# A decode-step layer on one core: gate rows in short pieces, decode states in a part of their own, flags between chains

## The chip, the cores and the metric

The kernel runs on one core of one Trainium2 chip. The metric is device time of that core in microseconds (us), lower is better. The core's engines run side by side, each through its own queue in order: TensorE (PE: matmuls; PEld is its weight load), VectorE (DVE), ScalarE (ACT), GpSimd (POOL) and SyncE (SP, which issues the DMA transfers).

## The reference

One inference step of a hybrid layer: a norm, one input projection, two groups of four heads side by side (mLSTM with gates and a running maximum, HGRN2), an output projection, then a SwiGLU feed-forward. It is computed for a prompt of 1024 positions and for 8 decode sequences of 4 positions, which carry states in and out. The part that the change touches, cut to its core:

```python
def _mlstm_chunk(carry, inp):            # one chunk of one head; carry = state
    C, n, m = carry
    q, k, v, ig, lf = inp
    ...
    F = jnp.cumsum(lf, axis=-1)
    a = F + m[..., None]
    D = jnp.where(mask, F[..., :, None] - F[..., None, :] + ig[..., None, :], -jnp.inf)
    m_t = jnp.maximum(a, jnp.max(D, axis=-1))
    w_inter = jnp.exp(a - m_t)
    W = jnp.exp(D - m_t[..., None])
    s_qk = jnp.einsum('bhtk,bhsk->bhts', q, k) * W
    num = w_inter[..., None] * jnp.einsum('bhtk,bhkv->bhtv', q, C) + jnp.einsum('bhts,bhsv->bhtv', s_qk, v)
    den = w_inter * jnp.einsum('bhtk,bhk->bht', q, n) + jnp.sum(s_qk, axis=-1)
    h = num / jnp.maximum(jnp.abs(den), jnp.exp(-m_t))[..., None]
    ...
    C_new = decay[..., None, None] * C + jnp.einsum('bhs,bhsk,bhsv->bhkv', w_last, k, v)

# around it: q, k = silu(causal conv of width 4 of the projection), lf = log_sigmoid of the f gate,
# out = sigmoid(o) * headnorm(h) * norm_g; for the prompt (state 0) and for decode (given state)
```

All of it is float32.

## The kernel before, in words

The 1056 columns (1024 prompt positions and 32 decode columns) are cut in three blocks: block 0 has 256 prompt columns and the 32 decode ones, blocks 1 and 2 have 384 each. The input projection is a list of *units*: one unit is one 128-row slice of the weights for one block. A float32 product is made of three matmuls on split operands (hi·hi L135, lo·hi L136, hi·lo L137), for 8 slices of the contraction. One such slice, three matmuls, is called a *triple* here, so a unit is 8 triples. For each head of the first group and each block there are units q, k, v, o; for the first head a unit for the gates too (at triples 0, 48 and 88). Then come the units of the second group, the output projection, the feed-forward.

Everything that is not a unit is written as a generator: the norm of the input (its multiplication of X by weight and factor is L228, the split into HI and LO is L229 and L225), the gates, the mixing chain of each head and block (`mix_a`), the decode part (`sample_a`). After every second triple and after each unit `hook()` moves each running generator one step on, where `yield n` says how many hooks to wait. All engines' instructions are written in the order in which these steps come, and each engine keeps that order. So the numbers in the tables (GAW for the gates, MAW for the mixing chains) and the `while ... yield 1` waits on entries of `done` set what stands ahead of what.

Names that the change and the prediction use (lines of before):

- `gates`: L301, L302 read the unit's result out of PSUM on ScalarE; L308 to L310 are the logarithm of the sigmoid (L310 needs another activation table, so a table load goes before it); L312 to L329 on VectorE, with the scans L317 and L319; L331 to L333 three exponentials; L334, L335 store rows to HBM; after more hooks the transposes L343 to L345 on TensorE, copied out by L346 and L347.
- `conv_evac`, q and k: L416, L417 read the unit's result (ScalarE), L435 and L437 or L439 keep the last columns, L445 three taps (VectorE), L449 a sigmoid (ScalarE), L450 the product (VectorE).
- `act_evac`: L469 and L470 for o, L472 for v.
- `mix_a`: L517, L519, L521 weights; L526, L530, L533 the scores and two transposes into three PSUM banks, pS, pK and pV; L540, L541, L544 read them; L549 the update of C, L557 and L559 its sum; L564 stores C; L570, L572 the output; L576 to L583 its norm; L588 a transpose back.
- the decode part: L708, L710 load ngS and wiS from HBM, L714 the scores, L717 to L722 their weights, L608 the load of a state, L612 and L613 transposes, L672 the state's product, L644 and L649 its update, L650 its store, L694 the last transpose.

PSUM gives four rotating banks `mx` to all chains and three banks `mm` to the units; a unit can start when its bank was read out. `finish(key)` runs hooks until a generator has ended, which puts the rest of its steps in one place: `conv_evac` does it for the chain of the block before.

## Time and profile before

| | us |
|---|---|
| median of 3 runs | 1394.06 (1393.78 to 1394.09) |
| the profiled execution | 1394.97 |
| its span, first to last instruction | 1392.9 |
| TensorE busy in it | 1337.1 (96%) |
| VectorE, ScalarE, GpSimd busy | 868.0, 558.6, 593.3 |
| mean granted TensorE clock | 0.982 |

A profile row of instructions reads: start, duration (both us), engine, line, operation, output <- input, shapes, how many. What stands in brackets is the time that the engine stood idle before it, and what ended that. A wait row reads: engine, tile and line that waited <- engine, tile and line it waited for, total us, times, longest. In the profiled execution the units of the first head run from the start to about 110 us, those of the other three heads of the first group to about 300 us; the units of the second group end near 550 us.

### The profile page before, as it was taken

How to read it: one execution, taken by the hardware profiler on the slowest of the kernel's cores; microseconds unless marked ns; L12 is line 12 of the kernel's file. 1: busy time of each engine (PE TensorE's matmuls, PEld its weight loads, DVE VectorE, ACT ScalarE, POOL GpSimd, SP SyncE). 2: the span in 40 equal slices, each digit the busy share in tenths (PEclk: the TensorE clock that was granted, in tenths of full speed). 3: DMA queues.
4: the chain of work that ended last, by engine and by line, in shares of the span. 5: the costliest groups of instructions: out<-in, count | busy, mean ns of one | idle time of the engine just before them, and what ended most of it. 6: DMA issues, size and time to landing. Idle time of an engine off the chain costs nothing.

```text
span 1392.9 us, 29377 instructions
## 1 busy us (share of the span) xinstructions
PE 1337.1 (96%) x11600; PEld 1306.0 (94%) x11600; DVE 868.0 (62%) x2060; ACT 558.6 (40%) x1315; POOL 593.3 (43%) x566
## 2 busy tenths in 40 slices
PE   7888999999999999999998999999999999999996
PEld 7778999899999998999998999999999999999995
DVE  7876667664555456644666667666765346777765
ACT  6554434233344334422435445554544341222232
POOL 5223212231222213222437666666666683444434
PEclk9999999999999999999999999999999999999997
DMA  6012122230101013553464666567654278878743
GB/s 226 23 38 60 66 63 74 87 109 17 49 32 49 32 49 116 149 160 109 163 202 171 211 227 250 204 216 254 218 210 168 78 261 321 300 278 295 278 152 125
DMA packets 108881, 212.11 MB, mean 152 GB/s; under 512 B 10800, under 2 KB 63560, under 8 KB 108232
## 3 DMA queue, kind: packets, MB, share of 16 engines
q1 hardware_dynamic: 108312, 209.98, 43.9%
q8 instruction: 91, 1.49, 0.4%
q14 instruction: 46, 0.38, 0.1%
q10 hardware_dynamic: 432, 0.27, 0.1%
HBM read 143.76 MB, written 66.45 MB: 151 GB/s over the span
## 4 chain that ended last, share of the span: by engine, by line
PE 78%; DVE 10%; ACT 4%; DMA 3%; issue 3%; SPq 1%; POOL 0%; POOLq 0%; DVEq 0%; ACTq 0%
PE mx L1260 16%; PE mm L135 9%; PE mm L1260 9%; PE mm L137 9%; PE mm L136 9%; PE mx L1483 8%; PE mm L1483 5%; PE so L1260 3%; PE mx L644 1%; PE mx L775 1%; PE so L1483 1%; DMA rg<-d_ff 1%; ACT HI L229 1%; DVE X L228 1%; DMA X<-d_x 1%
## 5 line engine op out<-in xcount | busy, mean ns | idle before, releaser
L135 PE MATMUL mm<-HI,whi 128*128 128x384 f32 (+2 forms) x1160 | 379.3, 327 | 6.6 <-ACT gA L302 2.9
L137 PE MATMUL mm<-HI,wlo 128*128 128x384 f32 (+2 forms) x1160 | 363.5, 313 | 1.1 <-POOL wlo L97 1.1
L136 PE MATMUL mm<-LO,whi 128*128 128x384 f32 (+2 forms) x1160 | 363.1, 313 | 0.4 <-POOL LO L225 0.2
L135 PEld LDWEIGHTS mm<-HI,whi 128*128 128x128 f32 x1160 | 221.4, 191 | 11.8 <-ACT gA L302 3.2
L137 PEld LDWEIGHTS mm<-HI,wlo 128*128 128x128 f32 x1160 | 221.3, 191 | 1.6 <-POOL wlo L97 1.6
L136 PEld LDWEIGHTS mm<-LO,whi 128*128 128x128 f32 x1160 | 221.7, 191 | 1.1 <-POOL LO L225 0.5
L97 POOL TENSOR_TENSOR wlo<-raw,whi 128x512 fp32r<-128x512 f32 x90 | 118.6, 1328 | 216.1 <-ACT whi L96 171.1
L1189 POOL TENSOR_TENSOR wlo<-S,whi 128x512 fp32r<-128x512 f32 x78 | 110.3, 1420 | 88.2 <-ACT whi L1188 85.2
L1260 PE MATMUL mx<-T,whi 128*128 128x264 f32 x640 | 118.2, 284 | 0.0
L1260 PEld LDWEIGHTS mx<-T,whi 128*128 128x128 f32 x640 | 99.0, 188 | 0.0
L1313 POOL TENSOR_TENSOR LO<-rg,HI 128x528 fp32r<-128x528 f32 x52 | 70.6, 1369 | 65.1 <-ACT HI L1312 65.1
L1260 PE MATMUL mx<-HI,whi 128*128 128x264 f32 x320 | 91.0, 285 | 0.0
L1260 PE MATMUL mx<-HI,wlo 128*128 128x264 f32 x320 | 90.9, 284 | 0.0
L1260 PE MATMUL mx<-T,wlo 128*128 128x264 f32 x320 | 90.9, 284 | 0.0
L1260 PE MATMUL mx<-LO,whi 128*128 128x264 f32 x320 | 90.7, 283 | 0.0
L1401 DVE TENSOR_TENSOR fh<-fr,fh 128x512 fp32r<-128x512 f32 x80 | 66.2, 828 | 35.0 <-ACT fh L1396 34.7
L1487 DVE TENSOR_TENSOR X<-X,mx 128x264 f32<-128x264 f32 x160 | 65.6, 425 | 26.5 <-PE mx L1483 25.9
L1188 ACT ACTIVATE whi<-S 128x512 fp32r<-128x512 f32 x80 | 50.3, 630 | 71.4 <-DVE S L1177 71.3
L1312 ACT ACTIVATE HI<-rg 128x528 fp32r<-128x528 f32 x52 | 32.3, 641 | 104.5 <-PE mx L1483 28.3
L1260 PE MATMUL mm<-HI,wlo 128*128 128x264 f32 x240 | 68.2, 284 | 0.0
L1260 PE MATMUL mm<-HI,whi 128*128 128x264 f32 x240 | 68.2, 284 | 0.0
L1260 PE MATMUL mm<-LO,whi 128*128 128x264 f32 x240 | 67.9, 283 | 0.0
(545 smaller groups left out, 3424.1 us busy)
## 6 DMA issues: line engine op xcount, KB each, us to landing
d_wf<-fh SPq DMA_DIRECT2D x60, 512.0 KB
rg<-d_ff SPq DMA_DIRECT2D x42, 528.0 KB
raw<-in_wA SPq DMA_DIRECT2D x31, 512.0 KB
whi<-d_wf SPq DMA_DIRECT2D x29, 512.0 KB
wlo<-d_wf SPq DMA_DIRECT2D x28, 512.0 KB
raw<-in_wgu SPq DMA_DIRECT2D x24, 512.0 KB
d_ff<-sg SPq DMA_DIRECT2D x40, 264.0 KB
rg<-in_wgu SPq DMA_DIRECT2D x20, 512.0 KB
```

Of the source, the lines that this page charges most:

```text
L97: (nc.gpsimd if pool else nc.vector).tensor_tensor(lo[:, s], raw[:, s], hi[:, s].bitcast(F32), op=OP.subtract)
L135: nc.tensor.matmul(ps[:, :n], wh, rh[:, k, :], start=(k == 0), stop=False)
L136: nc.tensor.matmul(ps[:, :n], wh, rl[:, k, :], start=False, stop=False)
L137: nc.tensor.matmul(ps[:, :n], wl, rh[:, k, :], start=False, stop=(k == nk - 1))
L1188: nc.scalar.activation(hi[:, s], t, AF.Copy)
L1189: (nc.vector if dve else nc.gpsimd).tensor_tensor(lo[:, s], t, hi[:, s].bitcast(F32), op=OP.subtract)
L1260: nc.tensor.matmul(ps[:, :QN], a[:, w], b_[:, kk, c], start=new and kk == 0 and x == 0, stop=kk == 3 and x == 2, skip_group_check=True)
L1312: nc.scalar.activation(h, src, AF.Copy)
L1313: (nc.vector if dve else nc.gpsimd).tensor_tensor(lw, src, h.bitcast(F32), op=OP.subtract)
L1401: nc.vector.tensor_tensor(lw, src, h.bitcast(F32), op=OP.subtract)
L1483: nc.tensor.matmul(ps[:, :QN], a[:, w], b_[k][:, cs], start=new and k == 0 and x == 0, stop=k == 1 and x == 2, skip_group_check=True)
L1487: nc.vector.tensor_tensor(y, y, ps[:, :QN], op=OP.add)
```

## The change

Four things change:

1. `gates`: more `yield`s cut the row work in short pieces, the table GAW is shortened, and the tiles gA and gB get two buffers. Blocks 1 and 2 no longer wait for the first head's chain of the block before at the start of their row work, only ahead of their stores.
2. `conv_evac` no longer finishes the chain of the block before for q of block 2 of the first head; for later heads it finishes the chain just before. Tiles v and go get a buffer more.
3. Chains of `mix_a` are ordered by `done` entries ("pOa", "pHa") and by `hold`, a flag that keeps others from taking banks between L526 and L544. `mix_b` gets such entries too.
4. `sample_a` leaves its state updates (L644, L649, L650) to `updates()`, which loads the eight states a second time (8 loads more on SyncE, 8 copies more on GpSimd, 8 products more on VectorE). It runs later and is finished ahead of the second decode part.
The matmuls are the same 10,286 in both, and TensorE's order is the same from about triple 526 on.

```diff
-    GAW = ((1, 6, 14), (2, 3, 6), (2, 3, 6))
+    GAW = ((1, 2, 10), (2, 2, 5), (2, 2, 5))
...
-            A, B, Cc = (mp.tile([36, 384], F32, tag=x, name=x) for x in ("gA", "gB", "gC"))
+            A, B, Cc = (mp.tile([36, 384], F32, tag=x, name=x, bufs=nb) for x, nb in (("gA", 2), ("gB", 2), ("gC", 1)))
...
-        while b and ("pS", 0, b - 1) not in done:
-            yield 1
         nc.scalar.activation(a, f, AF.Abs)
         nc.scalar.activation(a, a, AF.Exp, scale=-1.0)
+        yield 1
         nc.scalar.activation(a, a, AF.Ln, bias=1.0)
...
         nc.scalar.activation(wl, wl, AF.Exp)
+        while b and ("pS", 0, b - 1) not in done:
+            yield 1
         nc.sync.dma_start(d_bc[:, 0, o0:o0 + npr], ng)
...
-            if kind == "q" and b and (h or b == 2):
-                finish(("pS", h, b - 1))
+            if kind == "q" and h:
+                finish(("pS", (3 * h + b - 1) // 3, (3 * h + b - 1) % 3))
...
+    hold = [0]
+
     def mix_a(h, b):
...
+        while h + b and ("pOa", 3 * h + b - 1) not in done:
+            yield 1
...
         yield w[0]
+        while hold[0]:
+            yield 1
+        hold[0] = 1
         pS, pK, pV = bank(), bank(), bank()
...
+        while h + b and ("pHa", 3 * h + b - 1) not in done:
+            yield 1
         kt = tl("kt", 384, 1)
...
         nc.vector.scalar_tensor_tensor(W[:, :npr], pS[:, :npr], QS, W[:, :npr], op0=OP.mult, op1=OP.mult)
+        hold[0] = 0
...
                 nc.vector.tensor_scalar_mul(vm[:, 0:w], vt[:, 0:w], seqm[:, s:s + 1])
+                if w == 129:
+                    nc.gpsimd.tensor_copy(sts[s][:, :, 128:129], n_io[0][:, 4 * s:4 * s + 4, None])
                 yield 3
...
-            yield 3 if later is None else 2
+            yield 2
...
-                               o["Cs"], (nT, no), scol[:, 1:2], scol[:, 2:3])
-        nc.sync.dma_start(o["ns"], no)
+                               o["Cs"], (nT, no), scol[:, 1:2], scol[:, 2:3], later=("sua",))
...
         if ui == b0_first + 12 * (H - 1) + 8:
+            finish(("sua",))
             start(sample_b(), ("sb",))
```

How this moves instructions, at three places. Rows of the changed kernel carry its own line numbers: in `gates` L318, L321, L328, L329 are L317, L319, L325, L326 of before, and L332, L333 are L328, L329; in `conv_evac` L441, L443, L451, L456 are L435, L437, L445, L450; L476 is L470; in `mix_a` L556, L559, L573, L575, L580 are L541, L544, L557, L559, L564; L736, L738, L739 are L708, L710, L711.

First place, VectorE at triples 64 to 74: the gates of block 0 (tiles AT and C), the readout of o (go) and of q (st), then the norm of block 1 (L228). Before:

```order
L328 TENSOR_TENSOR AT_121<-C 4x256
L329 TENSOR_TENSOR AT_120<-AT_120,C 4x256
L470 TENSOR_SCALAR go<-go 128x288
L435 COPY raw<-hist 128x3
L437 COPY hist<-raw 128x3
L445 SCALAR_TENSOR_TENSOR st<-raw,vec,st 128x384 x3
L450 SCALAR_TENSOR_TENSOR st<-raw,st 128x384
L228 SCALAR_TENSOR_TENSOR X<-X,vec,mx 128x384 x2
L225 TENSOR_TENSOR LO<-X,HI 128x384
L228 SCALAR_TENSOR_TENSOR X<-X,vec,mx 128x384 x4
L225 TENSOR_TENSOR LO<-X,HI 128x384
```

Now, the row of go and what follows it:

```order
L476 TENSOR_SCALAR go<-go 128x288
L312 SCALAR_TENSOR_TENSOR AT_121<-AT_120,AT_121 4x288
L313 COPY C<-mcar 4x1
L318 SCALAR_TENSOR_TENSOR C<-ones,AT_121 4x128 x2
L321 SCALAR_TENSOR_TENSOR C<-AT_121,mcar,AT_120 4x256
L322 COPY mcar<-C 4x1
L328 TENSOR_TENSOR AT_120<-AT_120,C 4x256
L329 TENSOR_TENSOR C<-C 4x256
L441 COPY raw<-hist 128x3
L443 COPY hist<-raw 128x3
L451 SCALAR_TENSOR_TENSOR st<-raw,vec,st 128x384 x3
L456 SCALAR_TENSOR_TENSOR st<-raw,st 128x384
```

L312 to L326 of before have moved behind the readout of go, and L328 and L329 of before behind the conv's L450. A little further, where the last two of the eight L228 stood right behind the conv of k (ck), the rows now are:

```order
L225 TENSOR_TENSOR LO<-X,HI 128x384
L312 SCALAR_TENSOR_TENSOR gB<-gA,gB 4x384
L313 COPY gm<-mcar 4x1
L441 COPY raw<-hist 128x3
L443 COPY hist<-raw 128x3
L451 SCALAR_TENSOR_TENSOR ck<-raw,vec,ck 128x384 x3
L456 SCALAR_TENSOR_TENSOR ck<-raw,ck 128x384
L228 SCALAR_TENSOR_TENSOR X<-X,vec,mx 128x384
L318 SCALAR_TENSOR_TENSOR gC<-ones,gB 4x128 x3
L228 SCALAR_TENSOR_TENSOR X<-X,vec,mx 128x384
L321 SCALAR_TENSOR_TENSOR gm<-gB,mcar,gA 4x384
```

The gates of block 1 (tiles gA, gB, gC) stand among the norm's steps; in before they came after that block's L544.

Second place, VectorE in the second head, the conv of k and the readout of a chain's banks. Before:

```order
L445 SCALAR_TENSOR_TENSOR ck<-raw,vec,ck 128x384 x3
L450 SCALAR_TENSOR_TENSOR ck<-raw,ck 128x384
L583 TENSOR_SCALAR kt<-mx,sm 128x128 x2
L517 SCALAR_TENSOR_TENSOR W<-ngb,cols,cst 128x128 x3
L521 SCALAR_TENSOR_TENSOR qw<-cq,wib 128x384
L541 TENSOR_TENSOR kt<-mx,cols 128x384
L544 SCALAR_TENSOR_TENSOR W<-mx,W 128x384
```

Now:

```order
L441 COPY raw<-hist 128x3
L443 COPY hist<-raw 128x3
L451 SCALAR_TENSOR_TENSOR ck<-raw,vec,ck 128x384 x3
L456 SCALAR_TENSOR_TENSOR ck<-raw,ck 128x384
L556 TENSOR_TENSOR kt<-mx,cols 128x256
L559 SCALAR_TENSOR_TENSOR W<-mx,W 128x256
L608 SCALAR_TENSOR_TENSOR X<-mx,vec,go 128x384
```

The readout of the banks (L541 of before) now follows right behind the conv of another block's k unit, and TensorE's L549, which needs it, comes 8 triples behind that unit's end, not 20.

Third place, SyncE's queue ahead of the decode part. Before:

```order
L564 DMA out_Cp<-C 128x128
L487 DMA ngb<-d_bc 128x256
L488 DMA wib<-d_bc 128x256
L708 DMA ngS<-d_bc 32x32
L710 DMA wiS<-d_bc 128x32
```

Now:

```order
L493 DMA ngb<-d_bc 128x256
L494 DMA wib<-d_bc 128x256
L580 DMA out_Cp<-C 128x128
L736 DMA ngS<-d_bc 32x32
L738 DMA wiS<-d_bc 128x32
```

The store of C belongs to a chain that is written 20 triples later than before, and the loads of the decode part stand right behind it; on TensorE the decode part's scores (L714) now stand ahead of L526, L530 and L533 of the next chain.

More of the change, by code (lines that the diff above doesn't have):

```diff
@@ L238, in tl @@
     def tl(tag, n=384, bufs=2, dt=F32, p=128):
+        bufs = 3 if tag == "go" else bufs
         return mp.tile([p, n], dt, tag=tag, name=tag, bufs=bufs)
@@ L511, in mix_a @@
         while ("gc", b) not in done or ("cv", "k") not in done:
+            yield 1
+        while h + b and ("pOa", 3 * h + b - 1) not in done:
             yield 1
@@ L522, in mix_a @@
         yield w[0]
+        while hold[0]:
+            yield 1
+        hold[0] = 1
         pS, pK, pV = bank(), bank(), bank()
@@ L536, in mix_a @@
             nc.gpsimd.memset(ktm, 0.0)
+        while h + b and ("pHa", 3 * h + b - 1) not in done:
+            yield 1
         kt = tl("kt", 384, 1)
@@ L572, in mix_a @@
                 nc.tensor.matmul(pO[:, c, 0:129], qw[:, s], cin[c], start=False, stop=True)
+        done.add(("pOa", 3 * h + b))
         yield w[5]
@@ L588, in mix_a @@
             nc.tensor.transpose(pH[:, s], hn[:, s], ident)
+        done.add(("pHa", 3 * h + b))
         yield w[8]
@@ L610, in sample_core @@
         fetch(1)
+        while hold[0]:
+            yield 1
         pK, pV = bank(), bank()
@@ L640, in update @@
             st = sts[s]
+            while hold[0]:
+                yield 1
+            hold[0] = 1
             pUs = [bank(), bank()]
@@ L665, in updates @@
                 yield 3
+            if w == 129:
+                nc.sync.dma_start(o["ns"], n_io[1])
         for s in range(SEQS):
@@ L711, in sample_a @@
         nc.sync.dma_start(nT, i["n0T"])
+        while hold[0]:
+            yield 1
         pS = bank()
@@ L749, in mix_b @@
         q, f, k = S["qb", h, b], S["f", h, b], S["kb", h, b]
+        cid = atn[0]
+        while cid > 1 and ("pO", cid - 2) not in done:
+            yield 1
         AT, AD = ATs[atn[0] % 2], ADs[atn[0] % 2]
@@ L810, in mix_b @@
         yield 1
+        while samp and ("sa",) not in done:
+            yield 1
         nc.vector.copy_predicated(AD[:, :ncb, :], mk[0][:, None].to_broadcast([128, ncb, 32]),
@@ L819, in mix_b @@
         if samp:
-            while ("sa",) not in done:
-                yield 1
             nc.vector.tensor_copy(ss_["sk"][:, h, :], kB[:, 256:288])
@@ L876, in mix_b @@
         yield 1
+        while (("pHb", cid - 1) if cid else ("a", H - 1, 2)) not in done:
+            yield 1
         kt = tl("kt", 384, 1)
@@ L911, in mix_b @@
                 nc.tensor.matmul(pO[:, s], qp[:, s], cin[c], start=False, stop=True)
+        done.add(("pO", cid))
         yield 1
@@ L926, in mix_b @@
             nc.tensor.transpose(pH[:, s], hn[:, s], ident)
+        done.add(("pHb", cid))
         yield 1
```

8 lines of the change are left out of this document (5 added, 3 removed).

## The prediction

> **What bounds the kernel now.** I read three views in order. First the windows by stage: microseconds, busy time of each engine with its instruction count, the clock granted to TensorE, the DMA share and GB/s.
>
> ```profile
> 50.00:70.00 20.00, 14.35 (x76) 13.07 (x75) 16.25 (x36) 12.27 (x23) 4.67 (x6) 0.91 0.06 14
> 70.00:120.00 50.00, 39.40 (x235) 37.86 (x233) 34.80 (x85) 27.19 (x60) 16.04 (x20) 0.86 0.17 49
> 120.00:200.00 80.00, 78.88 (x534) 78.52 (x534) 52.09 (x153) 31.19 (x89) 18.62 (x29) 1.00 0.20 63
> 200.00:300.00 100.00, 98.34 (x706) 94.35 (x706) 68.53 (x198) 35.91 (x91) 28.88 (x58) 1.00 0.30 93
> ```
>
> TensorE (first column) sets the time everywhere. From 120 us on it is 98% busy at full clock, so nothing can be won there, but something can be lost. Only 50 to 120 us has slack: 16.3 us of idle, and a lowered clock. Second, the waits from 40 to 125 us: total, times, longest.
>
> ```profile
> PE mx L344 <- ACT gB L332: 4.1, 1, 4.1
> PE mx L572 <- DVE C L557: 3.7, 1, 3.7
> PE mm L135 <- ACT gA L302: 2.9, 1, 2.9
> PE mx L549 <- issue: 1.8, 1, 1.8
> PE mm L135 <- ACT st L417: 1.7, 1, 1.7
> PE mx L530 <- DVE X L228: 1.0, 1, 1.0
> ```
>
> Third, TensorE alone in windows of 2 us, where the second last figures but two give the clock:
>
> ```profile
> 52.00:54.00 2.00, 0.67 (x4) 1.00 0.00 0
> 60.00:62.00 2.00, 0.27 (x1) 1.00 0.44 110
> 64.00:66.00 2.00, 2.00 (x8) 0.50 0.00 0
> 82.00:84.00 2.00, 2.00 (x16) 0.50 0.74 145
> 110.00:112.00 2.00, 1.99 (x11) 0.50 0.66 151
> ```
>
> The 1.7 us wait near 52 us left the clock at 1.00; the idle of 2.9 us and more before 62, 82 and 110 us was each followed by windows at 0.50. A window at 0.50 loses 1 us, and each such spell spans two to three windows: I price it at 2 us.
>
> **The front, triples 72 to 128.** (A triple is L135, L136, L137 for one slice of the contraction; the k-th is counted from the start of the main loop.) The flags and pieces only change the order in which instructions are written, and each engine keeps that order. Here they put the steps of gates on VectorE and ScalarE ahead of work that TensorE waits for, and all later matmuls queue behind a waiting one. Rows of before:
>
> ```profile
> 51.54 0.45 DVE L312 SCALAR_TENSOR_TENSOR AT<-AT,AT 4x288 f32<-4x288 f32 x1 [2.24 <-ACT AT L310]
> 52.83 0.50 ACT L469 ACTIVATE go<-mx,hbo 128x288 f32<-128x288 f32 x1
> 53.99 0.41 DVE L326 TENSOR_TENSOR C<-C 4x256 f32<-4x256 f32 x1
> 55.33 0.31 DVE L470 TENSOR_SCALAR go<-go 128x288 f32<-128x288 f32 x1
> 55.89 1.92 DVE L445 SCALAR_TENSOR_TENSOR st<-raw,vec,st 128x384 f32<-128x384 f32 x3
> 58.47 0.56 DVE L450 SCALAR_TENSOR_TENSOR st<-raw,st 128x384 f32<-128x384 f32 x1 [0.65 <-ACT raw L449]
> 58.94 1.13 DVE L228 SCALAR_TENSOR_TENSOR X<-X,vec,mx 128x384 f32<-128x384 f32 x2
> 59.63 1.00 ACT L229 ACTIVATE HI<-X 128x384 fp32r<-128x384 f32 x2
> 61.11 0.57 ACT L302 ACTIVATE gA<-mm,vec 4x384 f32<-4x384 f32 x1
> ```
>
> Triple 72: L470 now stands ahead of L312 and cannot start before L469 ends at 53.33. So L312 starts at 53.66, L326 ends 2.86 later at 56.5, L445 runs 56.9 to 58.8, L450 ends at 60.0. Then come L328 and L329 (0.85 in before) and the two L228: 60.9 to 62.0. On ScalarE the three exponentials L331 to L333 (some 0.4 each) now stand between the two L229, so L302 ends near 64.9, not 61.7. TensorE, which ran dry at 58.8, idles 6.1 us in place of 2.9: +3.2.
>
> Triple 74: L530 needs the last of the eight L228 (its bank held their factor), and L533 needs L346. In before these wait 1.0 us in all, because the gates of the second block start only later:
>
> ```profile
> 74.02 1.28 ACT L310 ACT_TABLE_LOAD   x1
> 76.52 1.03 DVE L317 TENSOR_TENSOR_SCAN gC<-ones,gB 4x128 f32<-4x128 f32 x3
> 77.48 0.98 DVE L319 TENSOR_TENSOR_SCAN gm<-gB,mcar,gA 4x384 f32<-4x384 f32 x1
> 78.57 0.53 DVE L325 TENSOR_TENSOR gA<-gA,gC 4x384 f32<-4x384 f32 x1
> 80.29 0.55 DVE L329 TENSOR_TENSOR gA<-gA,gC 4x384 f32<-4x384 f32 x1
> ```
>
> Now they come first. ScalarE from 64.9: L229 0.5, L308, L309 0.5 each, L229 0.5, the load 1.3, L310 0.5, L229 0.5: 69.2. VectorE's L225 waits for that; ScalarE goes on with L229, L416, L417 to 70.9, which L445 waits for: to 72.9. A second table load ahead of L449 (1.28), L449 0.53, L450 0.56: 75.2. L228, three L317, L228: 77.4, and L530 goes. L319 to L329 take 78.4 to 80.8 and L346 releases L533 near 81. TensorE reached triple 74 at about 67 (two triples at half clock after 64.9) and stands some 13 us. It leaves triple 74 near 81 against 63 in before, of which 2 us are this chain's own transposes, which before makes later: +16.
>
> From there the change gives back. Before loses after triple 74 the waits for L530, L549 and L572 (6.5 us in the list above) and two spells of half clock: 10.5 us. The new order has its own half clock (2 to 3) and L572 still waits 2 us for L557, now behind L445 and L450. Shift at triple 118: 16 - 10.5 + 5 = +10; added up by absolute times (before passes it at 105.2, after 81 + 44 triples of 0.5 + some 8 of other matmuls and losses) it is +6. I take +7.
>
> Triple 118: L549 waits for L541, which stands behind the gates of the third block, whose L449 has a table load. Rows of that place in before, where a POOL subtraction (L97) runs beside the three scans, which take 3.13 us there and 1.03 above:
>
> ```profile
> 95.40 2.19 ACT L96 ACTIVATE whi<-raw 128x512 fp32r<-128x512 f32 x4
> 96.06 3.13 DVE L317 TENSOR_TENSOR_SCAN gC<-ones,gB 4x128 f32<-4x128 f32 x3
> ```
>
> After the k unit's end the chain L417, L445, load, L449, L450, L317 to L329, L541 is 10.5 us, TensorE has 7.6 us of work, and the four L96 ahead of L416 add up to 3: a stall of 3 to 10, I take 6.5. In its place goes the L344 wait of 4.1. Net +2. **Front: +9**, bounds +4 to +15.
>
> By the Trainium skill ("TensorE: Matmul & The Clock Gate", Part 1: The HAM clock gate) the clock falls only after an idle window of about 3.4 us; here 2.9 us was enough. By the page two stalls near 3 us that I charge with a half clock below would be free, which takes an estimated 4 us off the sum. The same notes ("ScalarE: Activation LUTs", What ACT_TABLE_LOAD costs) add about 1.38 us of drain to every load. The trace shows the next activation right behind the 1.28 us, and the row decides; by the page the two loads ahead of L530 would make it nearly 3 us worse, as an estimate.
>
> **The later chains, triples 150 to 440.** The order flags move each L549 from 20 triples behind its k unit to 8. It waits for L541, behind L445, L449 and L450 of that k unit:
>
> ```profile
> 91.85 0.56 DVE L541 TENSOR_TENSOR kt<-mx,cols 128x384 f32<-128x384 f32 x1 [0.25 <-PE mx L588]
> 219.57 3.03 DVE L445 SCALAR_TENSOR_TENSOR ck<-raw,vec,ck 128x384 f32<-128x384 f32 x3
> ```
>
> L416 to L541 is 1.1 + 1.9 + 0.6 + 0.6 + 0.6 with its gaps, 4.9 us; TensorE has 8 triples and L588, 4.75 us. So 0.15 us each at eight places without POOL, 1.4 us where L97 doubles a step (L445 3.03 in place of 1.92). POOL is busy about a quarter of this stretch: **+4.5**, bounds +1 to +11. Taken out are waits of before: 0.7 and 0.4 at L549 and L572 near 121 us, 0.6 at L694 near 300 us, and
>
> ```profile
> PE mx L572 <- DVE C L557: 1.6, 1, 1.6
> ```
>
> **-3.3.**
>
> **The decode part.** Its loads stand on SyncE's queue behind out_Cp of the third head's last chain, which now comes with the L549 at triple 336, not 316; and L533, now behind the decode part's products at triple 346, waits for the last L721:
>
> ```profile
> 229.78 0.83 PE L549 MATMUL mx<-vt,kt 128*128 128x129 f32 x6
> 232.33 0.34 SPq L564 DMA_DIRECT2D out_Cp<-C  x1
> 236.97 0.42 SPq L710 DMA_DIRECT2D wiS<-d_bc  x1
> 245.66 0.24 DVE L717 SCALAR_TENSOR_TENSOR sW<-ngS,scol,cst 128x32 f32<-128x32 f32 x1
> 247.52 0.19 DVE L722 SCALAR_TENSOR_TENSOR sq<-sq,wiS 128x32 f32<-128x32 f32 x1
> 81.21 0.34 SPq L487 DMA_DIRECT2D ngb<-d_bc  x1
> ```
>
> L549 to out_Cp 2.55, eight issues at 0.465, L717 to the last L721 1.85, and a landing that no row shows: at most the 4.8 us from L487 at 81.21 to the L517 that waited for it, at least nothing; I take 2.5. That is 10.6 us, and TensorE has 7 to 7.5: a stall of 3.2 and 2 of half clock, **+5**, bounds 0 to +9. At triple 362 L613 waits for L541 behind the conv of a k unit that ended two triples earlier: 4.9 - 1.5, some 3.3, and 2 of clock: **+5**, bounds +2 to +7. The L672 with two buffers of st, refilled 8 triples ahead (4 us), **+1.5**, bounds 0 to 6. The moved updates bring 8 loads of 256 KB, 8 copies on POOL and 8 products on VectorE into a stretch where DMA is a third busy and VectorE two thirds: **+1**, bounds -1 to +4. They lie beside TensorE's own work; without that cover the 8 products and 8 copies would cost 4 us. Behind them, from triple 526 on, the order is as before.
>
> **The sum**: 9 - 3.3 + 4.5 + 5 + 5 + 1.5 + 1 = +22.7 on the profiled execution's 1394.97, so 1417.7. The median of the runs is 0.9 lower than that execution: **1417 us**.
>
> **The rivals.** (1) The front alone: the short stalls from triple 150 on are taken up because VectorE and ScalarE run less behind than I chain them. Front +9, removed waits -3.3, and at most 4 of the rest, on 1394: 1400 to 1404, about 1402. For it speaks that the windows from 120 us show VectorE at 65 to 69%; against it that a queue in order passes on every delay. Chance 0.20. (2) The decode part decides: the loads of the state and of wiS queue up, so the landing takes its upper bound (+2.3), st its 6 us (+4.5) and the updates their 4 (+3), 10 more than my sum: 1427 and, with the upper bound of the chains, to 1440. For it speaks that two buffers leave 4 us for a load whose landing no row bounds below 4.8; against it that DMA is a third busy there. Chance for above 1432: 0.10. (3) The other side, faster: the pile-up at triple 88 to 96 was the dear place, and its price is L549 1.8, L572 3.7, L344 4.1 and two half-clock spells of 2, with 1.6 and 0.6 later: 18 us, 1376. It decides if the last L228 is done by 67 us, when TensorE reaches triple 74, that is if the gates of the second block do not get ahead of it on ScalarE and VectorE. The order speaks against it: L310's load and L445 both precede it. If only part of it comes, 1376 to 1391. Chance 0.10. (4) The stalls only move, sum within 2.8 us. Chance 0.05. My forecast, 1408 to 1432 around 1417, has 0.55.
>
> So slower by over 0.2% (2.8 us, about what these runs can tell from no change) has 0.20 + 0.10 + 0.55 = 0.85, within 0.05, faster 0.10. The range 1396 to 1436 leaves out (3), half of (2) and most of (4): 0.10 + 0.05 + 0.04, under 2 in 10.
>
> **What would show it.** Right: a wait of about 10 us for L228 near 67 us with L346 behind it, no wait at L344 near 106 us, a wait for L541 at triple 118, TensorE 7 to 11 us behind at triple 128, then waits for L541 of 0.2 to 1.4 us every 16 us, and one for L721 near 250 us. Wrong: TensorE busy from 67 to 77 us (then rival 3), the windows from 130 to 230 us at 99% (then rival 1), or a gain or loss behind 320 us, where the order is the same.

## The result, and the profile after

The changed kernel takes 1434.4 us (median of 4 runs, 1428.9 to 1435.6) against 1393.9 us: a ratio of 1.028, 95% interval 1.026 to 1.030. It is slower by 40 us. The forecast was 1417 us and slower. The measured time lies outside the forecast's own 1408 to 1432 us and 1.6 us inside the upper end of the stated range of 1396 to 1436. So the sign and most of the places were right, and the size was too small by 17 us. The profiled execution took 1433.76 us, its span is 1431.7.

The same stages in the profile of the changed kernel (us; busy time of PE, PEld, DVE, ACT, POOL with instruction counts; granted clock of TensorE; DMA):

```profile
50.00:70.00 20.00, 12.13 (x63) 11.01 (x61) 10.98 (x26) 13.16 (x23) 3.85 (x5) 0.84 0.07 14
70.00:120.00 50.00, 30.09 (x169) 28.88 (x169) 28.09 (x61) 20.80 (x40) 12.36 (x13) 0.81 0.12 35
120.00:200.00 80.00, 73.53 (x487) 72.36 (x488) 45.85 (x148) 29.20 (x83) 17.94 (x26) 0.95 0.19 60
200.00:300.00 100.00, 88.15 (x566) 85.47 (x565) 53.05 (x162) 30.39 (x85) 19.39 (x36) 0.95 0.17 52
300.00:400.00 100.00, 95.89 (x1041) 89.20 (x1041) 57.62 (x199) 35.23 (x107) 30.27 (x55) 1.00 0.31 93
```

TensorE now idles 20 us between 70 and 120 us, and it is no longer saturated behind 120 us either: 6.5, 11.9 and 4.1 us of idle in the next three windows, and a mean clock of 0.95 in two of them. VectorE is less busy than before in each of the first four windows, ScalarE in three of them. They have not become the bound; their work stands in the wrong order.

TensorE's waits from 40 to 150 us and, behind the dots, from 150 to 620 us (total, times, longest; lines are those of the changed kernel: L543 and L546 are L530 and L533 of before, L556 is L541, L565 is L549, L751 is L721, L632 is L612; L890, a product of the second group, is L858):

```profile
PE mx L543 <- DVE X L228: 10.1, 1, 10.1
PE mx L565 <- DVE kt L556: 9.4, 2, 8.6
PE mx L350 <- ACT AT L336: 3.7, 1, 3.7
PE mx L546 <- DVE cols L352: 3.6, 1, 3.6
PE mx L588 <- DVE C L573: 2.1, 1, 2.1
...
PE mx L890 <- DVE wib L834: 5.8, 6, 2.0
PE mx L565 <- DVE kt L556: 4.9, 5, 1.9
PE mx L546 <- DVE PB L751: 3.6, 1, 3.6
PE mx L565 <- POOL sv L482: 2.9, 2, 1.4
PE mx L632 <- ACT vt L555: 2.7, 1, 2.7
```

Each of the waits that the prediction walked through is there. The first row behind the dots is no new wait: the kernel before waits 4.0 us at the same line. To see what each costs in the end I compare positions and not only waits. TensorE's order of unit matmuls is the same in all kernels here, so the start of the first matmul (L135) of triple k can be compared between two traces, counted from each trace's first instruction. The difference to the kernel before is called the *lag*. It is set to 0 at triple 64, where the change begins to act, because executions differ by up to 2 us ahead of that. (Each of the two traces has 11,600 TensorE instructions, where the text on the change says 10,286 matmuls.) The table is worked out in this way from the traces of the runs (us):

| lag at triple | 72 | 80 | 96 | 112 | 128 | 208 | 336 | 368 | 448 | 524 |
|---|---|---|---|---|---|---|---|---|---|---|
| changed kernel | 3.0 | 18.0 | 11.4 | 8.4 | 15.2 | 17.6 | 25.2 | 31.3 | 30.7 | 38.9 |
| E1 gates back | 0.0 | 0.0 | -9.4 | -2.0 | 4.4 | 5.7 | 11.7 | 17.7 | 17.1 | 25.3 |
| E2 decode back | 3.0 | 17.0 | 10.5 | 7.4 | 13.7 | 16.2 | 23.7 | 31.4 | 43.5 | 44.8 |
| E3 flags alone | 0.0 | 0.0 | -9.4 | -1.3 | 4.4 | 5.7 | 13.2 | 18.9 | 32.1 | 33.4 |
| E4 norm first | 3.0 | 8.6 | 4.0 | 4.2 | 9.5 | 11.9 | 19.5 | 25.1 | 24.6 | 32.8 |
| E5 short tail | 3.0 | 17.9 | 11.4 | 8.4 | 15.1 | 17.5 | 25.2 | 24.1 | 25.9 | 30.7 |
| E6 decode alone | 0.0 | 0.0 | 0.0 | 0.0 | 0.0 | -0.1 | -0.1 | -0.5 | 1.6 | 6.4 |
| E7 repaired | 0.0 | 0.0 | -9.3 | -1.3 | 5.3 | 6.6 | 13.3 | 12.2 | 13.8 | 18.7 |
| E8 wait half filled | 3.0 | 18.2 | 13.2 | 10.1 | 16.3 | 18.8 | 26.3 | 31.7 | 31.2 | 39.4 |
| E9 later transpose | 0.0 | 0.0 | 0.6 | 0.6 | 0.5 | -0.1 | -0.1 | -0.6 | 0.7 | 5.5 |
| E10 tail of 4 | 0.0 | 0.0 | -9.4 | -2.8 | 2.9 | 2.2 | 6.0 | 6.0 | 6.4 | 11.2 |
| E11 both waits filled | 3.0 | 15.6 | 9.0 | 6.0 | 12.4 | 14.8 | 22.4 | 27.9 | 27.3 | 35.4 |

From triple 524 to the end the changed kernel's lag changes by less than 1 us: all of it is made between 55 and 411 us of its trace.

Two cautions go with the table. Each row is one execution: E8, which changes little, differs from the changed kernel by up to 1.8 us in it. And the lag also counts work that has only changed places. Over the whole stretch from triple 64 to 524 the changed kernel and the kernel before do the same matmuls, but at 112, for instance, 18 matmuls of a chain that the kernel before has done are still to come in the changed kernel.

The dearest place, triple 74, in the timeline of the changed kernel (start, duration, engine, line):

```profile
66.78 1.28 ACT L310 ACT_TABLE_LOAD   x1
68.07 0.52 ACT L310 ACTIVATE gB<-gB 4x384 f32<-4x384 f32 x1
...
69.17 0.56 DVE L225 TENSOR_TENSOR LO<-X,HI 128x384 fp32r<-128x384 f32 x1 [4.71 <-ACT HI L229]
71.45 1.92 DVE L451 SCALAR_TENSOR_TENSOR ck<-raw,vec,ck 128x384 f32<-128x384 f32 x3
73.44 1.28 ACT L455 ACT_TABLE_LOAD   x1 [2.72 <-DVE ck L451]
77.26 0.58 DVE L228 SCALAR_TENSOR_TENSOR X<-X,vec,mx 128x384 f32<-128x384 f32 x1
77.89 0.69 PE L543 MATMUL mx<-ident,ck 128*128 128x128 f32 x2 [10.13 <-DVE X L228]
81.33 0.55 DVE L333 TENSOR_TENSOR gA<-gA,gC 4x384 f32<-4x384 f32 x1
82.13 0.69 PE L546 MATMUL mx<-ident,ktm 128*128 128x128 f32 x2 [3.55 <-DVE cols L352]
```

The reader sees the chain of the prediction in order: the gates' logarithm with its table load, the norm's L225 that waited 4.7 us for ScalarE, the conv of k, a second table load for L455 (called a sigmoid above; the kernel writes it with a tanh), the last L228, and TensorE's L543 behind it; then the gates' last VectorE step and L546.

### The profile page after: what moved, and what is told of

The parts are those of the page before. It is cut to its first block, busy times and chain, and to the rows that moved or that the text cites. A ratio compares the mean times of both kernels' runs of the same rounds, so it can differ in the third digit from the quotient of the medians.

```text
span 1431.7 us, 29409 instructions
## 1 busy us (share of the span) xinstructions
PE 1344.0 (94%) x11600; PEld 1310.6 (92%) x11600; DVE 862.0 (60%) x2068; ACT 557.3 (39%) x1315; POOL 594.3 (42%) x574
## 3 DMA queue, kind: packets, MB, share of 16 engines
q8 instruction: 91, 1.49, 0.4%
## 4 chain that ended last, share of the span: by engine, by line
PE 75%; DVE 12%; ACT 6%; issue 3%; DMA 2%; POOL 0%; SPq 0%; POOLq 0%; DVEq 0%; ACTq 0%
PE mx L1296 16%; PE mm L1296 9%; PE mm L135 9%; PE mm L137 8%; PE mx L1519 8%; PE mm L136 8%; PE mm L1519 5%; PE so L1296 3%; DVE ck L451 2%; PE mx L807 1%; PE so L1519 1%; PE mx L667 1%; DMA rg<-d_ff 1%; ACT HI L229 1%; PE mx L565 1%
## 5 line engine op out<-in xcount | busy, mean ns | idle before, releaser
L135 PE MATMUL mm<-HI,whi 128*128 128x384 f32 (+2 forms) x1160 | 382.6, 330 | 3.2 <-ACT gA L303 1.3
L135 PEld LDWEIGHTS mm<-HI,whi 128*128 128x128 f32 x1160 | 223.8, 193 | 9.5 <-issue 3.2
L97 POOL TENSOR_TENSOR wlo<-raw,whi 128x512 fp32r<-128x512 f32 x90 | 117.1, 1314 | 178.1 <-ACT whi L96 175.4
L1523 DVE TENSOR_TENSOR X<-X,mx 128x264 f32<-128x264 f32 x160 | 65.5, 425 | 27.8 <-PE mx L1519 27.3
L504 POOL TENSOR_TENSOR sm<-sm,mhalf 128x3 f32<-128x3 f32 (+2 forms) x26 | 21.3, 818 | 144.1 <-DVE sm L499 50.4
```

The source lines that it names most:

```text
L97: (nc.gpsimd if pool else nc.vector).tensor_tensor(lo[:, s], raw[:, s], hi[:, s].bitcast(F32), op=OP.subtract)
L135: nc.tensor.matmul(ps[:, :n], wh, rh[:, k, :], start=(k == 0), stop=False)
L1523: nc.vector.tensor_tensor(y, y, ps[:, :QN], op=OP.add)
```

## The experiments

E1 to E3 take the change apart. **E1**, the gates as before:

```diff
-    GAW = ((1, 2, 10), (2, 2, 5), (2, 2, 5))
+    GAW = ((1, 6, 14), (2, 3, 6), (2, 3, 6))
...
+        while b and ("pS", 0, b - 1) not in done:
+            yield 1
         nc.scalar.activation(a, f, AF.Abs)
...
-        while b and ("pS", 0, b - 1) not in done:
-            yield 1
         nc.sync.dma_start(d_bc[:, 0, o0:o0 + npr], ng)
```

(and the pieces' `yield`s and the second buffers taken out).

> The changed kernel with the gates written as before (GAW, the pieces, the early wait for pS, one buffer of gA and gB); flags, decode part and conv rule stay changed. In the changed kernel TensorE is 15.0 us behind the kernel before at triple 128, 25.0 at triple 336, 38.8 at triple 524. Theory (the gates' steps stand ahead of the norm's L228 and of L541 on VectorE and ScalarE): the lag at triple 128 falls to 0 to 4 us, the later 24 us stay: 1416 to 1424 us. Rival (the front loss comes from the order flags and from the chain of block 0 no longer being finished early, not from the gates): the lag at triple 128 stays 12 to 15 us, 1430 us or more.

Measured: 1421.8 us, ratio 1.020 (1.017 to 1.022). The wait for L228 is gone and the lag at triple 128 is 4.4 in place of 15.2; the later 21 us stay. That is the theory, 0.4 us beyond its upper number. But the row holds a surprise: at triple 96 this kernel is 9.4 us *ahead* of the one before. Of that, 3.7 us are idle time and 3.0 us half clock that are gone between triples 80 and 96; the rest is 27 matmuls that come only behind triple 96. The likely cause is that the early `finish` ahead of block 2's q is left out (it runs hooks until the scores L526 of the chain before are written, not to the end of that chain); no run takes it out alone. TensorE then loses all of it again. Its waits, and ScalarE's queue at that place (lines of E1: L332 is L331 of before, L550 is L540, L560 is L549):

```profile
PE mx L560 <- ACT vt L550: 8.3, 1, 8.3
PE mx L583 <- DVE C L568: 3.1, 1, 3.1
...
107.56 1.28 ACT L332 ACT_TABLE_LOAD   x1
112.85 0.52 ACT L332 ACTIVATE gB<-gB 4x384 f32<-4x384 f32 x1 [4.01 <-DVE gB L329]
114.49 0.49 ACT L550 ACTIVATE vt<-mx 128x384 f32<-128x384 f32 x1
```

ScalarE stands 4 us at an exponential of the gates of block 2, which waits for VectorE's steps behind the scans, and the readout of vt that TensorE needs stands behind it.

**E2**, the decode part as before:

```diff
-                               o["Cs"], (nT, no), scol[:, 1:2], scol[:, 2:3], later=("sua",))
+                               o["Cs"], (nT, no), scol[:, 1:2], scol[:, 2:3])
+        nc.sync.dma_start(o["ns"], no)
...
-            yield 2
+            yield 3 if later is None else 2
...
-            finish(("sua",))
             start(sample_b(), ("sb",))
```

> The changed kernel with the decode part as before (state updates inside the loop, no second load of the states). Theory (the decode part is a loss of its own, 14 us from triple 336 to 524: the wait of pV for the decode weights, the waits at triple 362, the updates' work in the second group): lag at triple 336 unchanged at 25 us, lag at triple 524 at most 30 us: 1420 to 1426 us. Rival (the chains' new order makes that loss, whoever does the updates): lag at triple 524 stays above 35 us, 1431 us or more.

Measured: 1437.3 us, ratio 1.030 (1.027 to 1.033), not faster. The theory falls. The lag at triple 336 is the same as in the changed kernel within 1.5 us, at 524 it is 6 us more. The loss from 336 to 368 is there with the old decode part too (7.7), so it belongs to something else. Behind 448 the lag now grows by 1.3 in place of 8.2, but it grows by 10 between 416 and 448. The place is triple 440, where `finish(("sa",))` writes what is left of the decode part in one piece: between triples 432 and 448 TensorE does 24 state products (L672) and 24 update products (L644) more than in the kernel before, and stands still for 5.1 us:

```profile
PE so L700 <- POOL st L656: 2.9, 1, 2.9
PE mx L722 <- DVE sjunk L719: 2.2, 1, 2.2
```

(rows of E2 for 328 to 367 us: L700 is L672 of before, L722 is L694.) The late chains make the old decode part late, and what is late is done without cover. So with these chains the new decode part is a small gain by the traces; the intervals of the two ratios overlap.

**E3**, gates and decode part both as before (the edits of E1 and E2 together). What is left of the change are the flags, `hold`, the conv rule and the buffers of v and go.

> The changed kernel with gates and decode part both as before: the flags, the hold, the conv rule and the buffers of v and go are what is left of the change. Theory (three separate losses that add up): only the waits for L541 in the chains are left, 10 us, and 0 to 4 at the front: 1402 to 1409 us. Rival (the losses feed each other, each late queue making the next one late): below 1399 us. Other rival (the flags are the main loss): above 1415 us.

Measured: 1426.1 us, ratio 1.022 (1.020 to 1.025): the rival "the flags are the main loss". Flags, rule and buffers alone cost 32 us of the 40. The gates add 13 (E1 to the changed kernel) or 11 (E3 to E2), and the decode part takes 3 or 4 off (E2 to the changed kernel, E3 to E1; the intervals of both pairs overlap, the lag at 524 is lower by 6 and 8). These four were not run one by one; E5 shows a part of what the order flags do.

**E4**, only the place of the gates of block 1:

```diff
         while b == 0 and ("cv", "k") not in done:
             yield 1
+        while b == 1 and ("n1", 2) not in done:
+            yield 1
         nc.scalar.activation(a, f, AF.Abs)
```

> The changed kernel in which the gates of block 1 start their row work only when the norm of block 2 has written all its steps, so the eight L228 stand ahead of it; nothing else changes. Theory (place in the queue): the 10.1 us wait of TensorE for L228 falls to 3 us or less, the lag at triple 128 from 15 to 3 to 9 us: 1422 to 1428 us. Rival (the same VectorE and ScalarE work must be done before triple 118 anyway, so the stall only moves there): the lag at triple 128 stays 13 us or more, 1432 us or more.

Measured: 1428.0 us, ratio 1.024 (1.022 to 1.026). TensorE's waits:

```profile
PE mx L567 <- DVE kt L558: 13.3, 7, 7.6
...
PE mx L545 <- DVE X L228: 4.9, 1, 4.9
...
PE mx L352 <- ACT AT L338: 3.7, 1, 3.7
```

The wait for L228 falls from 10.1 to 4.9, not to 3 or less, and the wait for L346 (3.6) is gone; the lag at triple 128 falls by 5.7 us and is 9.5, half a us outside the expected 3 to 9. Place in the queue makes half of this wait and all of that for L346; the lag of 3.0 at triple 72, from block 0's gates behind the readout of go, is untouched by this edit. The stall at triple 118 stays (7.6 in place of 8.6), so the work has not simply moved there.

**E5**, one number of the chains' table:

```diff
-        (2, 1, 3, 1, 2, 2, 2, 6, 1))
+        (2, 1, 3, 1, 2, 2, 2, 3, 1))
```

> The changed kernel with one number of MAW changed: in the row for heads 2 to 4 the hooks between the norm of a chain (L583) and its transposes back (L588) are 3, not 6. The transposes set the flag pHa on which the next chain's readout (L541) waits, so L541 is written ahead of the next k conv and L549 goes back to its places in the kernel before from triple 284 on. Theory (the flag puts L541 behind the conv, and so delays every chain by 12 to 20 triples, which also brings the decode weights in front of pV): lag at triple 128 unchanged at 15 us, the waits for L541 between 200 and 336 gone, the wait for L721 at triple 346 gone, lag at triple 368 at 15 to 19 us instead of 31, the updates' part (448 to 524) still +6 to +8: 1415 to 1422 us. Rival (it is the decode part and its loads that make the losses from 336 on, wherever the chains stand): lag grows by 5 us or more between 336 and 368 as before, 1426 us or more.

Measured: 1424.1 us, ratio 1.022 (1.020 to 1.024). Both named waits are gone, that for L721 at triple 346 and that at 362: between triples 336 and 368 the lag now *falls* by 1.1 us, where it grew by 6.1. That part of the theory holds, and it takes the loss there from the decode part and gives it to the late chains. Between 208 and 336 nothing is won (7.7 and 7.6 us), since other waits stand in the place of those for L541:

```profile
PE mx L605 <- DVE kt L600: 3.5, 3, 1.4
PE mx L588 <- DVE C L573: 2.1, 1, 2.1
```

(rows of E5 for 200 to 265 us: L605 is the transpose L588 of before, L600 its norm L583; L588 and L573 are L572 and L557). Three hooks are too few for the norm through VectorE, ScalarE and GpSimd. And a wait of 4.6 us for L691 (sjunk) appears at the decode part's last transpose; it may be why the time is 2 us above the expectation.

**E6**, the decode part's change alone on the kernel before.

```diff
-                               o["Cs"], (nT, no), scol[:, 1:2], scol[:, 2:3])
-        nc.sync.dma_start(o["ns"], no)
+                               o["Cs"], (nT, no), scol[:, 1:2], scol[:, 2:3], later=("sua",))
```

(with the copy of the n column, the store of ns behind the updates and `finish(("sua",))`, as in the change).

> The kernel before with the decode part's change alone: the state updates in a part of their own with 8 more loads of the states; gates, chains and conv rule as before. Theory (the decode part by itself is no loss; its waits come from chains that are late): within 4 us of before, 1391 to 1398 us. Rival (second loads, copies and updates in the second group cost what the prediction's terms for triples 346 to 524 say): 1400 us or more.

Measured: 1401.1 us, ratio 1.0055 (1.0033 to 1.0076): the rival, by a little. The same edit that takes 3 us off among late chains costs 7 among punctual ones. More than half of that, by size, is one wait:

```profile
PE mx L698 <- DVE sjunk L695: 4.6, 1, 4.6
```

**E7**, a try at a repair: E1, the tail of 3, and the gates of block 2 behind the readout of block 1's chain.

```diff
-        while b and ("pS", 0, b - 1) not in done:
+        while b and (("pS", 0, 0) if b == 1 else ("kt", 0, 1)) not in done:
             yield 1
         nc.scalar.activation(a, f, AF.Abs)
...
         hold[0] = 0
+        done.add(("kt", h, b))
         yield w[2]
```

> The changed kernel with gates as in the run with the gates written as before, the short tail of 3 hooks, and one more wait: the gates of block 2 start their row work only when the chain of block 1 has written its readout (L540, L541, L544), so that readout no longer stands behind L331 to L333. Flags, hold and decode part stay changed. Theory: the wait of 8.3 us for vt at triple 124 goes, lag at triple 128 from +4 to -6 to 0 us, the waits for L541 go, what is left is the updates' part: 1392 to 1402 us. Rival (gates of block 2 come too late for their own chain, and the wait moves to L344 or L549 of the next chain): lag at triple 152 at +3 us or more, 1404 us or more.

Measured: 1413.9 us, ratio 1.013 (1.010 to 1.016): the rival. The wait of 8.3 us for vt is gone, and in its place TensorE's L572 (L584 here) waits nearly as long for the next step of the same chain, L559 (L571 here):

```profile
PE mx L584 <- DVE C L571: 7.4, 1, 7.4
```

The gates of block 2 hold VectorE for 8 us in one piece (105.4 to 113.4 us in E1). At both places where they were put between triples 96 and 128, the chain's next step waits for them; the lag at triple 128 is 5.3 with this repair and 4.4 without.

**E8** fills part of TensorE's stand at triple 74 with transposes that nobody reads.

```diff
         done.add(("pS", h, b))
+        if (h, b) == (0, 0):
+            dm = bank("so")
+            for _ in range(30):
+                nc.tensor.transpose(dm[:, 0:128], ident, ident)
```

> The changed kernel with 30 more transposes on TensorE (identity by identity into the unused bank so, read by nobody) between L526 and L530 of the first chain, where TensorE otherwise stands idle for 10 us waiting for L228. Nothing that anyone waits for moves. Theory (an idle stretch halves the clock that is granted after it, and that costs time of its own): the granted clock is at 1.00 again by 78 us, triples 74 to 80 lose 0 to 1 us to the clock in place of 2.5, the lag at triple 80 falls from 17.8 to 14 to 16 us: 1430 to 1433 us. Rival (the clock of this stretch follows something else than TensorE's own idling): the clock stays at 0.50 until about 87 us and the time at 1434 us or more.

Measured: 1432.1 us, ratio 1.028 (1.026 to 1.030). Inconclusive: the 30 transposes ended 4 us before the wait did; the clock rose to 1.00 at 72 us and fell again at 79. It did show what one costs (14 in 1.49 us at full clock), from which the next run is sized.

**E11** fills both waits: 68 of them ahead of L530 and 26 between L530 and L533.

> As the run with 30 more transposes, but with 68 of them between L526 and L530 and 26 between L530 and L533 of the first chain (0.106 us each at full clock, by that run), so that TensorE is busy through nearly all of the two waits for L228 and L346. Theory (the granted clock follows TensorE's own idling, in stretches of 3.4 us): full clock from about 72 us on, no half clock between 75 and 90 us, triples 74 to 80 some 2.5 us shorter, the lag at triple 80 at 14 to 16.5 us in place of 17.8, the later lag lower by as much. Rival: the clock stays low until about 87 us and the lag at triple 80 at 17 us or more.

Measured: 1430.1 us, ratio 1.025 (1.022 to 1.027). TensorE alone in windows of 2 us (busy time, instructions, granted clock), first the changed kernel, then E11:

```profile
74.00:76.00 2.00, 0.00 (x0) 0.50 0.00 0
84.00:86.00 2.00, 2.00 (x8) 0.50 0.27 70
86.00:88.00 2.00, 2.00 (x10) 0.64 0.56 130
```

```profile
74.00:76.00 2.00, 2.00 (x21) 1.00 0.00 0
84.00:86.00 2.00, 2.00 (x13) 1.00 0.22 63
86.00:88.00 2.00, 2.00 (x15) 1.00 0.42 137
```

In the same 2 us TensorE does 13 and 15 matmuls in place of 8 and 10. The lag at triple 80 falls by 2.4 us and stays lower by 2.3 to 3.5 us from there on. The half clock behind a stall is a cost of its own, about what the prediction put on it (2 us a spell). The intervals of the two ratios overlap, so for the whole kernel this difference rests on the traces.

**E9**, E6 with the decode part's last transpose later:

```diff
         nc.vector.tensor_scalar_mul(hn, pO[:, 0:128], sm[:, 2, 0:1])
-        yield 1
+        yield 4
         pH = bank()
```

> The kernel before with the decode part's change alone, and the last transpose of a decode part (L694) three hooks later behind the VectorE step that it needs (L691). Theory (of the 7 us that the decode part alone costs, 4.6 us of wait at this one place and a half-clock spell of 2.5 us are the whole): 1391.5 to 1396 us, no wait at L694 above 0.5 us. Rival (the moved updates and second loads are a cost of their own): 1397.5 us or more.

Measured: 1401.8 us, ratio 1.0053 (1.0033 to 1.0073): the rival. The wait for L691 is gone; the updates' first product (L644) now waits in its place:

```profile
PE mx L644 <- DVE svm L660: 3.6, 1, 3.6
```

The lag grows by 2.6 us between triples 336 and 400 and by 4.8 between 448 and 524, where the moved products now stand. From triple 336 to 524 the matmuls are the same as in the kernel before, so what moved cancels, and what is left is idle time (+3.3 us) and half clock (+2.6). So the decode part's change has a price of its own in the kernel before, 5.5 us by the lag and 7.7 by the medians, and it is not this one wait.

**E10** joins what helped: E1, a tail of 4 hooks (long enough for the norm, short enough that L541 is written ahead of the next k conv in most chains), and E9's later transpose.

> The changed kernel with the gates written as before, 4 hooks in place of 6 ahead of L588 in heads 2 to 4, and L694 three hooks later; flags, hold and decode part stay changed. Theory (parts add: front +4 as with the gates written as before, chains +2 to +4, triples 336 to 368 -1, no wait at L694, updates +5): lag at triple 524 +6 to +11 us: 1400 to 1405 us. Rival (each change of place only hands the wait to the next step, as in the repaired kernel's front): 1411 us or more.

Measured: 1407.5 us, ratio 1.011 (1.009 to 1.013); its profiled execution's lag at triple 524 is 11.2, 0.2 us above the expected span of values. It lies between theory and rival. The chains from triple 128 to 336 cost 3.1 us in place of 10.0, and between 336 and 368 nothing. It is the fastest kernel here with flags, but no version beat the kernel before.

## Why the prediction was right, and where it was short

**The sum.** The prediction had +9 for the front, +3.4 for the chains and +10.3 for triples 336 to 524; measured are 15.2, 10.0 and 13.7. All three parts were too small, and none made up for another. Over the whole stretch, in which the matmuls are the same, TensorE idles 31.8 us more than in the kernel before and loses 5.4 us more to half clock. That the time still lies in the range is in part luck: the prediction gave the band above 1432 us to rival (2) with a chance of 0.10, and what that rival needs did not happen (below).

**The front: place right, size +9 predicted, +15.2 measured.** Triple 72: +3.2 predicted, +3.0; what ends the wait is L302 of before, as predicted (it ends at 64.6, 64.9 predicted), with a wait for an exponential (3.7 us, L350 above) ahead of it that the prediction did not have. Triple 74: waits of 10.4 and 2.6 ("some 13 us") predicted, 10.1 and 3.6 measured. All stalls that the prediction put between triples 64 and 128 add up to 27.6 us (6.1, 13, 2 and 6.5); the trace has 29.6. So the stalls were nearly right, and what was mis-sized is the way from them to the sum. From triple 74 to 118 the prediction counted the shift in two ways, +10 and +6, and took +7. Measured is +8.4 at triple 112 with 18 matmuls still to come, about 2.5 us by an estimate from L565 above (six in 0.9 us), so +10 was the better of the two. At triple 118 a stall of 6.5 was predicted and 8.6 measured; with these 18 matmuls and 0.7 us more of half clock +2 became +6.8 (15.2 - 8.4). L318, the scans, stood under POOL's L97 again (from 115.22 for 2.71 us) and took 2.99 us:

```profile
115.21 2.99 DVE gC L318 x3
118.21 0.92 DVE gm L321
121.53 0.57 DVE kt L556
```

(rows of the critical chain: start, length, what.) E1 and E4 show that the order of the gates makes this part. What the prediction did not see is E1's other half: with the gates as before, the rest of the change is 9.4 us ahead at triple 96, at the place that rival (3) described, and each place of block 2's gates that was tried gives it back by triple 128.

**The chains: +4.5 less 1.1 predicted (the waits of before near 121 us), +10.0 measured** (triples 128 to 336). The mechanism was right, L549 behind the conv of a k unit; the term was mis-sized. TensorE's idle at the seven places between triples 144 and 336 is 0.8, 0.3, 1.9, 1.4, 0.3, 1.9, 1.4: I had said 0.2 to 1.4 each. The two of 1.9 are the k units of block 2, where L445 runs beside POOL's L97 and takes 2.76 us in place of 1.93; the prediction had such places, at 1.4. The two of 0.3 are the k units of block 1, without L97. The other three I had priced like blocks of 384 columns, with 4.75 us of cover. For chains whose k unit is a block 0 unit the cover is eight triples of 288 columns, and behind L423 stand L427, three more taps (L454) and GpSimd copies. One such place in the changed kernel:

```profile
198.24 0.58 ACT L423 ACTIVATE ck<-mm,b,vec 128x288 f32<-128x288 f32 x1
201.46 0.46 DVE L456 SCALAR_TENSOR_TENSOR ck<-raw,ck 128x288 f32<-128x288 f32 x1 [0.57 <-ACT raw L455]
201.83 0.55 DVE L556 TENSOR_TENSOR kt<-mx,cols 128x384 f32<-128x384 f32 x1
202.26 0.21 POOL L482 COPY sv<-v 128x32 f32<-128x32 f32 x1
202.53 0.91 PE L565 MATMUL mx<-vt,kt 128*128 128x129 f32 x6 [1.44 <-POOL sv L482]
```

A spell of half clock near 245 us (1.7) makes up the rest.

**The decode part: places and path right, put down to the wrong edit.** The wait of L533 for L721 was predicted at 3.2 and is 3.6; that at triple 362 was predicted at 3.3 and is 2.7, each followed by a half clock. The path to L721 is the predicted one: the critical chain runs from out_Cp (266.23) over the loads on SyncE's queue to the landing of the last ngS,

```profile
270.38 2.82 DMA ngS<-d_bc
```

2.8 us where I took 2.5. The prediction charged both waits to the decode part. E5 removes both with one number of the chains' table, E2 leaves them in place with the old decode part (its lag from 336 to 368 is 7.7). They belong to the flags, which write L549 of most chains 20 triples later and so bring the decode part's short steps ahead of the next chain's transposes. The term for st (+1.5) did not come: no matmul of the first decode part waits for st in the changed kernel.

The sum over triples 336 to 524 was predicted at +12.5 less 2.2 and measured at +13.7. That is 8.6 us more idle time on TensorE and 3.1 us more lost to half clock; 12 matmuls of a chain that came ahead of triple 336 in the kernel before are the rest. The moved products cancel. The 64 products of the updates (L644, L667 in the changed kernel) stood ahead of triple 416 in the kernel before and stand behind it now, so the lag falls where they are gone and grows where they come, as the last 8.2 between triples 448 and 524 mostly does (48 products, with 2.4 us of idle). First the kernel before from 250 to 300 us, then the changed kernel from 340 to 400 us:

```profile
L644 PE MATMUL mx<-svm,ktm 128*128 128x129 f32 x64 | 9.3, 288 | 0.0
```

```profile
L667 PE MATMUL mx<-svm,ktm 128*128 128x129 f32 x40 | 5.3, 274 | 0.0
```

To price the moved work at nothing was right for the sum. What was missed are short waits: behind triple 448 (2.4 us), and at the last transpose (1.9 us for L691, where the prediction took a wait of 0.6 out).

**Two rules weighed.** By the Trainium skill ("TensorE: Matmul & The Clock Gate", Part 1: The HAM clock gate) stalls near 3 us would have been free. The trace decides against that: the stalls of 3.6 and 2.7 us near 275 and 288 us were each followed by a window at 0.50,

```profile
276.00:278.00 2.00, 2.00 (x7) 0.50 0.01 2
290.00:292.00 2.00, 2.00 (x8) 0.50 0.00 0
```

though the page's picture of free-running windows of about 3.4 us agrees: every half-clock spell in these traces lasts 3.41 us or a multiple of it, but for the last of each trace, which the trace's end cuts off. The traces say more. I cut all 13 of them, from 55 to 420 us, into stretches of 3.41 us that line up with the changes of the clock. The clock fell after every stretch at full clock in which TensorE idled 1.82 us or more, and after none in which it idled 1.78 us or less. So the length of a stall does not decide alone: the changed kernel has the same stall of 1.87 us at 181.6 and at 241.6 us; the first is shared by two stretches (1.46 us in one) and cost no clock, the second lies in one and was followed by half clock from 244.5 us. The Trainium skill's page "ScalarE: Activation LUTs" (What ACT_TABLE_LOAD costs) would add a drain to each load; the two loads quoted above took 1.28 us and the activation followed within 0.02.

**The rivals and the signs.** (1), the front alone, is refuted: the lag grows by 23.7 us behind triple 128. (2), the decode part decides, named nearly the right time (1432 to 1440) for a wrong reason: it needs a landing near 4.8 us, and it was 2.8, and a loss of 6 us at st, where there was none. Its terms also reach only 1433 or 1434 us (1427 and 6.5 for the chains' upper bound), not 1440; the prices listed for (3) add up to 15.8 us, not 18. (3) had its gain for some 30 triples where the gates are as before (E1), and lost it. Two of the prediction's signs failed: TensorE was 15.2 us behind at triple 128, not 7 to 11, and there is a loss behind 320 us, 9 us from triple 400 on. That sign had the wrong time in it: the order is the same only from triple 526 on, which starts at 374 us in the kernel before and at 413 in the changed one, and from there on the lag stays.

**What stays open.** The flags, `hold`, the conv rule and the buffers were not run one by one, so which of them makes the gain at triple 96 is argued. Whether a place of block 2's gates exists that keeps it was tried at two places only, and the short waits behind triple 448 were not followed to their cause.

## What to carry to other kernels

In a kernel whose bound engine is fed by in-order queues, a change that only reorders is priced by asking, for each moved step, what now stands behind it and how much cover the bound engine has at that place; the cover must be taken from the smallest tile that comes by, not from the usual one. A wait is not the property of the instruction that waits: take each edit out alone before charging it, since the same edit cost 7 us in one order and, by the traces, saved some in another. And compare two traces by position in the bound engine's stream; the lag by position shows gains that are lost again later, which no list of waits shows. Count the other work in the same stretch with it: where work has only moved, the lag falls at one place and grows at another by as much, and neither is a gain or a loss.

## What the runs showed that was not expected

- The granted clock moves in steps of 3.4 us: in the changed kernel it was low from 63.6 to 87.5 us, seven such steps, through a stretch in which TensorE did work from 64 to 68 us. Work that nobody needs, put into a wait, raised the clock behind it and made the rest of the kernel 2.3 to 3.5 us earlier (E11).
- Each move of one block of small steps (the gates of block 2) moved the stall from L344 (4.1 us in the kernel before) to L541 (8.6), to the readout of vt (8.3) and to L559 (7.4): at none of these places was it hidden.
